# Sums of squares of the differential heads on column tiles, halvings spaced apart, and one head's norm factors taken later

## The chip, the core and the metric

The kernel runs on one core of a Trainium2 chip. The core has a matrix engine (TensorE, PE in the profile; PEld is its weight load), VectorE (DVE), ScalarE (ACT), GpSimd (POOL) and SyncE (SP), which here only starts DMA transfers. Each engine works through its own instructions in order, and engines wait for each other by semaphores. The metric is device time in microseconds (us) of one execution, as the median of several runs. The profile comes from one further execution.

## The reference

One decoder layer on 512 tokens of 1024 channels. The part that matters here is the differential attention: four heads, each with two softmax maps whose difference weights the values, followed by an RMS norm over the 128 value channels of that head.

```
p = softmax(scores)                               # (b, h, 2, q, s)
a = p[:, :, 0] - lam * p[:, :, 1]
out = einsum('bhqs,bshe->bqhe', a, v)             # 128 channels a head
out = rmsnorm(out, subln_g) * (1.0 - lam_init)
```

Beside it runs a modulation: `mod = silu(c) @ w_ada + b_ada` gives six rows of 1024 numbers (shift, scale, gate for each half of the layer). Before the attention there is a modulated norm and one input projection; a sliding-window attention, sigmoid gates, branch projections, an output projection, and a gated MLP with a short convolution complete the layer.

## The kernel before, in words

Matrix products of full precision are made of three products of halves of numbers (high x high, high x low, low x high; `mm3`, lines 130 to 132). Weights come in raw, ScalarE casts the high part and VectorE subtracts it for the low part (L126 and L127 in `split`).

The attention stages are written as a hand-set order on TensorE and POOL (a `manual_schedule` block); a scheduler orders DVE, ACT and SP by priorities and its own estimates of time. The clock of that written order is `fill(n)`: it emits n *ticks*, each three products of 512 columns for whatever projection is due (pq, pk and pw for queries, keys and values of later heads; pga and pgd for the gates; pA and pB for the branches). `after(n, fn)` has fn emitted n ticks later, `flush(kind)` emits what has been laid by under a name.

A differential head h goes through four query blocks n = 0 to 3. `diff_scores` makes the scores sd of one or two blocks on row tiles of 64 rows, `diff_softmax` the maps, `diff_transpose` turns them (td) and stores them as high and low parts (aTh, aTl). With all four turned, `diff_values` makes the head's output od, 128 channels by 512 tokens, channels on the partitions. ScalarE stores its squares (sq) and a scaled copy (of). The norm then has three steps, laid by for heads 0 to 2 and emitted during the next head:

- `stats` (list "sum", at n = 2): the sum of squares over the 128 channels for each token. Each of four blocks of 128x128 squares is loaded as weights and multiplied by one column of ones, so the sums (pss) come out with tokens on the partitions, one column a block. VectorE scales them by the softmax sum (dr) and makes a mean (ms); POOL raises it to the power -1/2 (L193).
- `end` (list "end", at n = 3): VectorE refines the root and makes the norm factors drs.
- `turn_norm` (list "norm", at n = 0 of the head after): four transposes (rb) spread the factors over the channels, VectorE multiplies, and a split stores the result outd.

For head 3 the same steps follow by counts of ticks (STAT_LAG, END_LAG, NORM_LAG). Head 2's factors are turned after the loop over blocks, between four ticks and od of head 3.

The modulation rows are computed beside this: `ada_rows` loads pieces of w_ada (ra) every eighth tick, and VectorE adds them up (arow), 128 partial sums of 1024 numbers for each of four rows. `ada_sum` then adds the partitions by halving: POOL starts seven DMA transfers that add the upper half of the partitions onto the lower (64, 32, ... 1), each after the one before has landed, and an eighth that writes the row to mod_rows in memory. They are emitted HALVE_LAG ticks apart. Rows 1 and 2 are read back into a tile m (L1079, on SP), which is turned on TensorE (pm) M2_LAG ticks after it was planned, and VectorE makes coefficients c of it. Behind the load of m on SP stand the last branch weights (wbd) and the output weights (wo), which VectorE multiplies by the first gate (L1135).

PSUM tiles named with `tbank` (tag t) share two buffers: pv, td, pss, rb and pm are all of this kind.

Of the kernel before, what the change touches and what calls it, by code (L numbers as in the profile page):

```python
# [8 lines left out]
F32 = mybir.dt.float32  # L9
# [5 lines left out]
P = 128  # L15
# [3 lines left out]
NT = S // P  # L19
# [9 lines left out]
ADA_AHEAD = 2  # L29
HP = 100000  # L30
ST = 6
HALVE_LAG = 6
ADA_EVERY = 8
ADA_EASY = 20

ROW_BEHIND = {0: -3, 4: -2}
ADA_START = 4
V_LAG = 13
M2_LAG = (48, 60)
STAT_LAG = 10  # L40
END_LAG = 3
NORM_LAG = 16
SWA_FILL = (2, 2, 5, 2, 2, 2, 2, 3)
DIFF_FILL = (3, 2, 4, 2)
# [14 lines left out]
def kernel(  # L59
# [22 lines left out]
    nc = tc.nc  # L82
# [3 lines left out]
    def pool(name, bufs=1, space=None, stack=ctx):  # L86
        kw = {} if space is None else {"space": space}
        return stack.enter_context(tc.tile_pool(name=name, bufs=bufs, reuse_waits="tile", **kw))
# [6 lines left out]
    def bank(tag, bufs, shape, name, dt=F32):  # L95
        return ps.tile(shape, dt, tag=tag, bufs=bufs, name=name)
# [4 lines left out]
    def sbank(name, shape=(P, S)):  # L101
        return bank("s", 3, list(shape), name)

    def tbank(name, shape=(P, S)):
        return bank("t", 2, list(shape), name)
# [28 lines left out]
    def mm3_rows(groups):  # L134
        for a, b, start, stop in ((0, 0, True, False), (0, 1, False, False), (1, 0, False, True)):
            for o, lhs, rhs in groups:
                nc.tensor.matmul(o, lhs[a], rhs[b], start=start, stop=stop)  # L137


    ones = cpool.tile([P, P], F32, name="ones")  # L140
    nc.gpsimd.memset(ones, 1.0)
    ident = cpool.tile([P, P], F32, name="ident")
# [347 lines left out]
    ap = pool("att", stack=at)  # L490
# [51 lines left out]
    def prefetch():  # L542
        while units and len(loaded) < 2:
            load, run = units.pop(0)
            loaded.append((load(), run))

    def fill(n):
        for _ in range(n):
            if not current:
                prefetch()  # L550
                if loaded and due[0]:
                    due[0] -= 1
                    wts, run = loaded.pop(0)
                    current.append(run(wts))
                    if tick[0]:
                        prefetch()
            if tick[0] == 7:
                prefetch()
            if current:
                try:  # L560
                    next(current[0])
                except StopIteration:
                    current.clear()
            for e in list(later):
                e[0] -= 1
                if e[0] <= 0:
                    later.remove(e)
                    e[1]()
            tick[0] += 1
            if tick[0] >= ADA_START and tick[0] % ADA_EVERY == 0:  # L570
                next(ada, None)

    beside = {"sum": [], "end": [], "norm": [], "turn": []}

    def after(n, fn):
        later.append([n, fn])

    def flush(*kinds):
        for kind in kinds:
            while beside[kind]:  # L580
                beside[kind].pop(0)()
# [148 lines left out]
    def diff_scores(*ss):  # L730
        ops = []
        for s in ss:
            h, n = divmod(s, NT)
            t = heads[h]
            w = (n + 1) * P
            if n == 0:
                firsts[h] = [sbank(f"sd{h}_{m}", (P, 2, 256)) for m in range(2)]
            sps = [
                firsts[h][m][:, n, :w] if n < 2 else (vbank if n + m == 4 else sbank)(f"sd{h}_{n}_{m}")[:, :w]
                for m in range(2)  # L740
            ]
            mm3_rows([
                (
                    sps[m],
                    [t[64 * m : 64 * m + 64, b, n * P : (n + 1) * P] for b in range(2)],
                    [t[64 * m : 64 * m + 64, 2 + b, :w] for b in range(2)],
                )
                for m in range(2)
            ])
            ops.append((s, sps, w))  # L750
        for s, sps, w in ops:
            h, n = divmod(s, NT)
            mx = ap.tile([P, 2], F32, tag="dmx", bufs=3, name=f"dmx{h}_{n}")
            pm = []
            for m in range(2):
                st = ap.tile([P, w], F32, tag="st", bufs=ST, name=f"sd{h}_{n}_{m}")
                with tc.high_priority(offset=HP):
                    maxima.append(nc.vector.tensor_tensor_reduce(
                        st, sps[m], ddf[:, 512 - w : 512], 1.0, -3e38, ALU.add, ALU.max, mx[:, m : m + 1]
                    ))  # L760
                pm.append(st)
            scored[s] = mx, pm
# [39 lines left out]
    def diff_values(h):  # L802
        t, (aTh, aTl) = heads[h], aTs[h]
        o = vbank(f"od{h}")
        for k in range(NT):
            q0 = k * P
            mm3(
                o[:, q0:], t[:, 4, k * P : (k + 1) * P], t[:, 5, k * P : (k + 1) * P],
                aTh[:, k * AW + q0 : k * AW + 512], aTl[:, k * AW + q0 : k * AW + 512],
                k == 0, k == NT - 1,  # L810
            )
        sq = ap.tile([P, S], F32, tag="tmp", bufs=2, name=f"sq{h}")
        of = ap.tile([P, S], F32, tag="of", bufs=2, name=f"of{h}")
        nc.scalar.activation(sq, o, AF.Square)
        nc.scalar.activation(of, o, AF.Copy, scale=sublnc)

        def stats():
            pss = tbank(f"pss{h}", (P, NT))
            for n in range(NT):
                nc.tensor.matmul(pss[:, n : n + 1], sq[:, n * P : (n + 1) * P], ones[:, 0:1], start=True, stop=True)  # L820
            rs, r0, r2 = (ap.tile([P, NT], F32, tag=t, bufs=2, name=f"{t}{h}") for t in ("drs", "dr0", "dr2"))
            nc.vector.reciprocal(r0, sums[h][:, 0])
            nc.vector.tensor_mul(r2, r0, r0)
            nc.vector.tensor_mul(r2, r2, pss)
            half = rstd_start(r2, NT, P, ap)

            def end():
                rstd_end(rs, *half, NT, ap)
                nc.vector.tensor_mul(rs, rs, r0)

            if h < 3:
                beside["end"].append(end)
            else:
                after(END_LAG, end)

            def turn_norm():
                rb = tbank(f"rb{h}")
                for n in range(NT):
                    nc.tensor.transpose(rb[:, n * P : (n + 1) * P], rs[:, n : n + 1].to_broadcast([P, P]), ident)
                with tc.high_priority(offset=HP):  # L840
                    nc.vector.tensor_mul(of, of, rb)
                split(outd[0][:, h], outd[1][:, h], of)

            if h < 3:
                beside["norm"].append(turn_norm)
            else:
                after(NORM_LAG, turn_norm)

        if h < 3:
            beside["sum"].append(stats)  # L850
        else:
            after(STAT_LAG, stats)


    mod_rows = tc.dram_tile([4, D], F32, name="mod_rows")
# [39 lines left out]
    def ada_sum(idx, whole):  # L895
        def step(n):
            if n:
                nc.gpsimd.dma_start(whole[0:n], whole[n : 2 * n], accum_op=ALU.add)  # L898
                after(HALVE_LAG, lambda: step(n // 2))
            else:  # L900
                nc.gpsimd.dma_start(mod_rows[idx : idx + 1], whole[0:1].rearrange("o a n -> o (a n)"))

        after(1, lambda: step(P // 2))
# [98 lines left out]
    for s in range(4 * DIFF_HEADS):  # L1002
        h, n = divmod(s, NT)
        if s in (4, 8):
            due[0] += 3
        elif s == 12:
            due[0] += 4
        ahead = s == 1
        fill(DIFF_FILL[1] - ahead)
        nxt = (s + 1, s + 2) if n % 2 and s < 15 else ()  # L1010
        if nxt:
            diff_scores(*nxt)
        if n == 3:
            with tc.issue_after(maxima[-1].ins):
                flush("end")
        if n == 1:
            diff_transpose(s)
        fill(DIFF_FILL[2] + ahead)
        if n == 2:
            flush("sum")  # L1020
        elif n == 0:
            flush("norm")
        if n != 1:
            diff_transpose(s)
        diff_softmax(*nxt)
        if n == 0 and h:
            diff_values(h - 1)
            fill(DIFF_FILL[3])
    due[0] += 2 * (KT - 4)
    fill(4)  # L1030
    flush("norm")
    diff_values(DIFF_HEADS - 1)
    while due[0] or current:
        fill(1)
    at.close()
# [52 lines left out]

    after(M2_LAG[0], load_m2)
    after(M2_LAG[1], turn_m2)  # L1090

# [270 lines left out]
    ssq, r2, xns = {}, {}, {}  # L1362
# [609 lines left out]
```

## Time and profile before

| what | us |
|---|---|
| median of the 3 runs shown (lowest, highest) | 690.01 (689.94, 692.77) |
| profiled execution, its own time | 691.2 |
| span of its instructions | 689.4 |
| TensorE busy | 677.5 (98%) |
| VectorE busy | 563.9 (82%) |
| ScalarE busy | 382.2 (55%) |
| GpSimd busy | 100.1 (15%) |

A row of the timeline has a start and a length in us from the span's start, the engine, the line of the source, the operation, what it writes and reads, its form, how many were merged into the row, and in brackets how long the engine was idle before it and what released it. Ends of products are modelled and overlap: a product with 512 columns is shown as 0.39 us long though the next one starts 0.23 us after it, so what a thing costs on TensorE is read from start to start. A window's row has the length, then busy time and instructions of PE, PEld, DVE, ACT and POOL, the TensorE clock granted, the share of the DMA engines, and GB/s.

The attention stages that the change touches lie between 110 and 235 us; from 235 to 308 us come gates and branches, then the output projection, and from 350 us the MLP.

### The profile page before, as it was taken

Reading aid. Unit: us, or ns where it says so; the run is one execution under the profiler, and the core shown is the slowest. Engines: PE = TensorE matmul, PEld = TensorE weight load, DVE = VectorE, ACT = ScalarE, POOL = GpSimd, SP = SyncE. Lnnn points to the kernel's source line nnn. Section 1 sums busy time; section 2 is a strip of 40 time slices with the busy share of each in tenths; the row PEclk is TensorE's granted clock in tenths of the full one; section 3 lists DMA queues with packets and bytes.
Section 4 is the critical chain, followed back from the end, with each engine's and each line's share of the span. In section 5 each row is a group of like instructions: output and inputs, shape, how many; then the busy total and the mean of one; then the engine's idle time right before and its main releaser. Section 6 shows DMA issues by size and latency. Waiting matters only on the chain.

```text
span 689.4 us, 11101 instructions
## 1 busy us (share of the span) xinstructions
PE 677.5 (98%) x4139; PEld 593.0 (86%) x4139; DVE 563.9 (82%) x1073; ACT 382.2 (55%) x678; POOL 100.1 (15%) x121
## 2 busy tenths in 40 slices
PE   8999999999989999999999999999999999999995
PEld 5887787888878888788899999999999999888885
DVE  5999775988775676793589988888888999979997
ACT  7676674546442323333377656655555666656665
POOL 3000000021012101111030011112110102440300
PEclk9999999999999999999999999999999999999998
DMA  9995412565455687569635788777979647995903
GB/s 306 351 295 180 131 61 76 166 167 157 139 145 160 215 256 201 170 175 327 216 67 119 181 209 191 170 168 216 208 212 220 155 161 182 196 205 144 168 1 122
DMA packets 116934, 123.89 MB, mean 180 GB/s; under 512 B 4983, under 2 KB 93848, under 8 KB 116880
## 3 DMA queue, kind: packets, MB, share of 16 engines
q1 hardware_dynamic: 97038, 95.11, 43.1%
q0 software_dynamic: 19648, 27.79, 23.8%
q8 instruction: 32, 0.52, 0.3%
q10 hardware_dynamic: 194, 0.28, 0.1%
q14 instruction: 22, 0.18, 0.1%
HBM read 118.97 MB, written 2.11 MB: 176 GB/s over the span
## 4 chain that ended last, share of the span: by engine, by line
PE 95%; DMA 2%; DVE 1%; ACT 0%; issue 0%; SPq 0%; POOL 0%; POOLq 0%; ACTq 0%
PE up L1300 32%; PE dc L1916 15%; PE a L393 5%; PE pgd L130 2%; PE pgd L131 2%; PE pgd L132 2%; PE oc L1356 2%; PE oc L1360 2%; PE oc L1357 2%; PE pga L130 2%; PE pga L132 2%; PE pga L131 2%; PE pq L130 1%; PE pw L130 1%; PE sd L137 1%; DMA adaw<-in_w_ada_dram 1%
## 5 line engine op out<-in xcount | busy, mean ns | idle before, releaser
L1300 PE MATMUL up<-t,m_whi 128*128 128x256 f32 x512 | 93.1, 283 | 0.0
L1300 PEld LDWEIGHTS up<-t,m_whi 128*128 128x128 f32 x512 | 79.9, 192 | 0.0
L1300 PE MATMUL up<-t,m_wlo 128*128 128x256 f32 x256 | 72.4, 283 | 0.0
L1300 PE MATMUL up<-bh,p_whi 128*128 128x256 f32 x232 | 65.7, 283 | 0.0
L1300 PE MATMUL up<-bl,p_whi 128*128 128x256 f32 x232 | 65.7, 283 | 0.0
L1300 PE MATMUL up<-bh,p_wlo 128*128 128x256 f32 x232 | 65.7, 283 | 0.0
L898 POOL DMA_DIRECT2D arow<-arow x28 | 22.6, 807 | 254.0 <-DVE sd L783 123.9
L1300 PEld LDWEIGHTS up<-t,m_wlo 128*128 128x128 f32 x256 | 49.2, 192 | 0.0
L1209 POOL DMA_DIRECT2D s<-in_w_up_dram x21 | 26.9, 1354 | 140.9 <-DMA s<-in_w_up_dram 58.9
L1300 PEld LDWEIGHTS up<-bh,p_whi 128*128 128x128 f32 x232 | 44.5, 192 | 0.0
L1300 PEld LDWEIGHTS up<-bl,p_whi 128*128 128x128 f32 x232 | 44.5, 192 | 0.0
L1300 PEld LDWEIGHTS up<-bh,p_wlo 128*128 128x128 f32 x232 | 44.5, 192 | 0.0
L890 DVE SCALAR_TENSOR_TENSOR arow<-ra,cs,arow 128x512 f32<-128x512 f32 x56 | 41.8, 748 | 0.4
L1237 ACT CAST m_whi<-s 128x1024 fp32r<-128x1024 f32 x31 | 32.5, 1049 | 11.1 <-DVE s L1231 6.3
L1241 DVE TENSOR_TENSOR m_wlo<-s,m_whi 128x1024 fp32r<-128x1024 f32 x31 | 37.8, 1219 | 0.0
L1300 PE MATMUL up<-t,p_whi 128*128 128x256 f32 x176 | 32.2, 283 | 0.0
L1300 PEld LDWEIGHTS up<-t,p_whi 128*128 128x128 f32 x176 | 27.5, 192 | 0.0
L1307 ACT ACTIVATE gT<-a,cv 128x512 f32<-128x512 f32 x22 | 17.7, 814 | 16.9 <-DVE a L1342 15.9
L1237 ACT CAST p_whi<-wa 128x1024 fp32r<-128x1024 f32 x18 | 18.8, 1043 | 12.5 <-PE up L1300 12.5
L193 POOL TENSOR_TENSOR r<-ms,mhalf 128x1 f32<-128x1 f32 (+1 forms) x16 | 13.1, 820 | 83.0 <-DVE ms L191 64.8
L1241 DVE TENSOR_TENSOR p_wlo<-wa,p_whi 128x1024 fp32r<-128x1024 f32 x18 | 22.0, 1223 | 3.8 <-ACT p_whi L1237 3.8
L1300 PE MATMUL up<-t,p_wlo 128*128 128x256 f32 x88 | 24.9, 283 | 0.0
(486 smaller groups left out, 2061.6 us busy)
## 6 DMA issues: line engine op xcount, KB each, us to landing
ra<-in_w_ada_dram SPq DMA_DIRECT2D x32, 512.0 KB, 4.3
wa<-in_w_up_dram SPq DMA_DIRECT2D x22, 512.0 KB, 4.6
s<-in_w_up_dram SPq DMA_DIRECT2D x21, 512.0 KB, 5.2
s<-in_w_up_dram POOLq DMA_DIRECT2D x21, 512.0 KB, 7.1
adaw<-in_w_ada_dram SPq DMA_DIRECT2D x12, 512.0 KB, 7.3
w<-in_w_in_dram SPq DMA_DIRECT2D x12, 512.0 KB, 4.9
a<-in_w_up_dram SPq DMA_DIRECT2D x11, 512.0 KB, 4.9
b<-in_w_down_dram SPq DMA_DIRECT2D x10, 512.0 KB, 4.9
```

The lines of the kernel that those rows point to most:

```text
L130: nc.tensor.matmul(o, lh, rh, start=start, stop=False)
L131: nc.tensor.matmul(o, lh, rl, start=False, stop=False)
L132: nc.tensor.matmul(o, ll, rh, start=False, stop=stop)
L393: nc.tensor.matmul(acc6[i], lhs[:, i * P : (i + 1) * P], rhs[k], start=k == 0 and p == 0, stop=last and p == 2)
L890: nc.vector.scalar_tensor_tensor(ac, r[:, a], cc, ac, ALU.mult, ALU.add)
L898: nc.gpsimd.dma_start(whole[0:n], whole[n : 2 * n], accum_op=ALU.add)
L1209: nc.gpsimd.dma_start(dst, upblock(*blk), accum_op=ALU.add)
L1237: nc.scalar.copy(W[J, name][0], R[J, SRC[name]])
L1241: nc.vector.tensor_sub(lo, R[J, SRC[name]], hi.bitcast(F32))
L1300: nc.tensor.matmul(o[u], w[:, k, cu], b[:, k], start=name in ("p1", "m5", "p2") and k == 0 and x == 0, stop=k == 3 and x == 2, skip_group_ ...
L1307: nc.scalar.activation(grow(j), av[J][:, u], AF.Identity, bias=cv[:, 66 + j : 67 + j], scale=cv[:, 44 + j : 45 + j])
L1916: nc.tensor.matmul(bank2[u][:, sl], a[:, q, cu], b[:, q, sl], start=first_mm and x == 0, stop=last_mm and x == 2, skip_group_check=name no ...
```

## The change

Sums of squares. `add_rows` is new: four products with a 128x32 block of ones as weights and 128 columns of squares, each on its own column tile of 32 columns (`tile_position`), so that token block g's sums stand on partitions 32g to 32g+31 of psr. ScalarE copies psr to ssrow; `stats` turns that tile once (pss) and reads columns 0, 32, 64 and 96. For heads 0 to 2 `add_rows` is emitted at n = 1 ahead of the scores, the turning where `stats` stood. For head 3 `add_rows` follows od by 7 ticks and the turning comes 3 ticks later, where one count of 10 stood before.

Third head's factors. `end` of head 2 is emitted after the loop and six ticks, then od of head 3, and `turn_norm` of head 2 eight ticks later.

Halvings. The first two gaps between the seven halvings grow from 6 ticks to 10 and 7. M2_LAG grows by 6.

```
-HALVE_LAG = 6
+HALVE_LAG = (10, 7, 6, 6, 6, 6, 6)
+LAST_NORM = 8
-M2_LAG = (48, 60)
-STAT_LAG = 10
+M2_LAG = (54, 66)
+STAT_LAG = 7
+TURN_LAG = 3
...
+        row = ap.tile([P, P], F32, tag="ssrow", name=f"ssrow{h}")
+        def add_rows():
+            pr = tbank(f"psr{h}", (P, P))
+            for g in range(4):
+                gs = slice(32 * g, 32 * g + 32)
+                nc.tensor.matmul(
+                    pr[gs], ones[:, gs], sq[:, g * P : (g + 1) * P], start=True, stop=True, tile_position=(0, 32 * g)
+                )
+            with tc.high_priority(offset=HP):
+                nc.scalar.copy(row, pr)
+            if h < 3:
+                beside["sum"].append(stats)
+            else:
+                after(TURN_LAG, stats)
...
-            pss = tbank(f"pss{h}", (P, NT))
-            for n in range(NT):
-                nc.tensor.matmul(pss[:, n : n + 1], sq[:, n * P : (n + 1) * P], ones[:, 0:1], start=True, stop=True)
+            pss = tbank(f"pss{h}", (P, P))
+            nc.tensor.transpose(pss, row, ident)
...
-            nc.vector.tensor_mul(r2, r2, pss)
+            with tc.high_priority(offset=HP):
+                nc.vector.tensor_mul(r2, r2, pss[:, 0:P:32])
...
-            beside["sum"].append(stats)
+            beside["row"].append(add_rows)
         else:
-            after(STAT_LAG, stats)
+            after(STAT_LAG, add_rows)
...
-                after(HALVE_LAG, lambda: step(n // 2))
+                after(HALVE_LAG[7 - n.bit_length()], lambda: step(n // 2))
...
+            if n == 1:
+                flush("row")
             diff_scores(*nxt)
-        if n == 3:
+        if n == 3 and nxt:
...
-    fill(4)
-    flush("norm")
+    fill(6)
+    flush("end")
     diff_values(DIFF_HEADS - 1)
+    after(LAST_NORM, lambda: flush("norm"))
```

Where this moves instructions. POOL, the powers (r) of the second, third and fourth head and the halvings (arow) of the second modulation row, before:

```order
L193 TENSOR_TENSOR r_2065<-ms,mhalf 128x4
L898 DMA arow_1680<-arow_1680 64x1024
L898 DMA arow_1680<-arow_1680 32x1024
L193 TENSOR_TENSOR r_2327<-ms,mhalf 128x4
L898 DMA arow_1680<-arow_1680 16x1024
L898 DMA arow_1680<-arow_1680 8x1024
L898 DMA arow_1680<-arow_1680 4x1024
L193 TENSOR_TENSOR r_2476<-ms,mhalf 128x4
```

and now:

```order
L195 TENSOR_TENSOR r_2072<-ms,mhalf 128x4
L919 DMA mod_rows<-arow_1051 16x1x64
L916 DMA arow_1680<-arow_1680 64x1024
L195 TENSOR_TENSOR r_2338<-ms,mhalf 128x4
L916 DMA arow_1680<-arow_1680 32x1024
L916 DMA arow_1680<-arow_1680 16x1024
L916 DMA arow_1680<-arow_1680 8x1024
L916 DMA arow_1680<-arow_1680 4x1024
L195 TENSOR_TENSOR r_2498<-ms,mhalf 128x4
```

The third head's power stands ahead of the halving of 32 partitions instead of behind it, and the second head's ahead of the write of the first row.

TensorE behind the last block of head 3, where head 2's factors were turned (rb) and od begins, before:

```order
L130 MATMUL pga_2375<-hThA,wga_h 128x512
L131 MATMUL pga_2375<-hTlA,wga_h 128x512
L132 MATMUL pga_2375<-hThA,wga_l 128x512
L839 MATMUL rb_2392<-ident,drs_2319 128x128 x4
L130 MATMUL od_2400<-aTh_2177,qkv_1879 128x512
```

and now the place where rb of head 2 stands, eight ticks behind od, one tick behind the sums of head 3:

```order
L825 MATMUL psr_2464<-sq_2423,ones 32x128 x4
L132 MATMUL pga_2460<-hThA,wga_h 128x512
L133 MATMUL pga_2460<-hTlA,wga_h 128x512
L134 MATMUL pga_2460<-hThA,wga_l 128x512
L857 MATMUL rb_2473<-ident,drs_2330 128x128 x4
```

Od follows gate products directly, and no four transposes of factors lie ahead of it.

VectorE near 284 us, where the coefficients c are made and the first output weights are multiplied by the gate, before:

```order
L1084 COPY c_2662<-pm_2961 128x40
L127 TENSOR_TENSOR mg1l<-tdall,mg1h 128x512
L1085 TENSOR_TENSOR c_2662<-c_2662 128x16
L890 SCALAR_TENSOR_TENSOR arow_2717<-ra_6_2907,cs,arow_2717 128x512
L1086 SCALAR_TENSOR_TENSOR c_2662<-c_2662 128x8
L1135 TENSOR_TENSOR wo_3147<-wo_3147,g1b 128x1024
```

and now:

```order
L1156 TENSOR_TENSOR wo_3163<-wo_3163,g1b 128x1024
L129 TENSOR_TENSOR mg1l<-tdall,mg1h 128x512
L908 SCALAR_TENSOR_TENSOR arow_2732<-ra_6_2922,cs,arow_2732 128x512
L1156 TENSOR_TENSOR wo_3170<-wo_3170,g1b 128x1024
L1105 COPY c_2678<-pm_2997 128x40
```

The first product with wo is ahead of what stood before it, and a second one is ahead of the copy of pm.

More of the change, by code (lines that the diff above doesn't have):

```diff
@@ L571, in fill @@
                 next(ada, None)
-    beside = {"sum": [], "end": [], "norm": [], "turn": []}
+    beside = {"row": [], "sum": [], "end": [], "norm": [], "turn": []}
     def after(n, fn):
```

## The prediction

> **What bounds the kernel now.** I read the page's busy shares and its chain first, then the waits of TensorE, then the stretch around the one long wait.
>
> ```profile
> PE 677.5 (98%) x4139; PEld 593.0 (86%) x4139; DVE 563.9 (82%) x1073; ACT 382.2 (55%) x678; POOL 100.1 (15%) x121
> PE 95%; DMA 2%; DVE 1%; ACT 0%; issue 0%; SPq 0%; POOL 0%; POOLq 0%; ACTq 0%
> ```
>
> TensorE is the bound: 95% of the chain is its own work. A change gains by less TensorE time or by closing one of its gaps. The longest gap in the view of waits is one that the change touches:
>
> ```profile
> PE rb L839 <- DVE drs L829: 1.9, 1, 1.9
> ```
>
> The timeline around it (start, length, engine, line, instruction), cut to the chain's rows:
>
> ```profile
> 196.04 0.88 POOL L898 DMA_DIRECT2D arow<-arow  x1 [20.01 <-DVE dr L822]
> 198.84 0.16 DVE L189 TENSOR_SCALAR ms<-dr 128x4 f32<-128x4 f32 x1
> 201.07 0.60 PE L797 MATMUL td<-ident,sd 128*128 128x128 f32 x4
> 203.08 0.78 POOL L898 DMA_DIRECT2D arow<-arow  x1 [6.16 <-DMA arow<-arow]
> 203.62 1.29 POOL L193 TENSOR_TENSOR r<-ms,mhalf 128x4 f32<-128x4 f32 x1
> 204.06 0.39 PE L132 MATMUL pga<-hThA,wga_l 128*128 128x512 f32 x1
> 205.43 0.68 DVE L499 TENSOR_TENSOR aTl<-td,aTh 128x512 fp32r<-128x512 f32 x1
> 206.32 0.71 PE L839 MATMUL rb<-ident,drs 128*128 128x128 f32 x4 [1.87 <-DVE drs L829]
> 207.26 0.63 PE L131 MATMUL od<-aTl,qkv 128*128 128x512 f32 x1
> 207.69 0.63 PE L132 MATMUL od<-aTh,qkv 128*128 128x512 f32 x1
> 210.21 0.44 PE L130 MATMUL pga<-hThA,wga_h 128*128 128x512 f32 x1
> ```
>
> The third head's mean square (ms) is ready at 199.0, but its power on POOL starts at 203.62: ahead of it in POOL's order stands the row's second halving (203.08), which waits 6.16 us for the first to land. So rb, and TensorE behind it, starts at 206.32. The product at 204.06 takes its place for 0.23 us (the spacing of its neighbours), so the gap is 206.32 - 204.29 = 2.03 us.
>
> It costs more than itself. Behind it the products od follow each other at 0.43 us (207.26 to 207.69). The head before reads:
>
> ```profile
> 182.82 0.60 PE L839 MATMUL rb<-ident,drs 128*128 128x128 f32 x4
> 183.60 0.39 PE L131 MATMUL od<-aTl,qkv 128*128 128x512 f32 x1
> 183.84 0.39 PE L132 MATMUL od<-aTh,qkv 128*128 128x512 f32 x1
> 185.23 0.45 PE L130 MATMUL pga<-hThB,wga_h 128*128 128x512 f32 x1
> ```
>
> There the spacing is 0.24, and from rb to the next gate product pass 2.41 us, against 3.89 behind the gap: 1.48 us more for the same work. The windows tell why (their last columns: granted clock, DMA share, GB/s):
>
> ```profile
> 198.00:204.20 6.20, 6.20 (x32) 5.00 (x31) 3.41 (x7) 2.97 (x4) 1.12 (x2) 1.00 0.96 277
> 206.30:210.10 3.80, 3.78 (x16) 3.51 (x16) 3.77 (x6) 0.62 (x1) 0.94 (x2) 0.56 0.41 67
> 210.10:214.00 3.90, 3.90 (x19) 3.27 (x19) 1.18 (x2) 1.99 (x4) 0.69 (x1) 0.99 1.00 281
> ```
>
> The granted clock is 1.00 before the gap, 0.56 for 3.8 us behind it, then 0.99.
>
> **The change, part by part.** *Halvings and the third head's norm.* POOL now has this power behind the issue of the first halving (196.04 plus 0.88) and ahead of the second. It can start with ms at 199.0, so the norm factors come some 4 us earlier, and rb asks for them eight ticks behind od, some 8 us later. The gap loses its cause: -2.03, and -1.48 of slow clock, together **-3.51 us**. The second halving waits for the first one's landing until 203.08 in any case, so the power (1.29) in front of it is free. The first two heads' powers now stand ahead of one halving and of the write of the first row, and hold these back by what they wait for ms. That row was done at 166.41 and the next halving started only at 196.04: slack of 29 us covers it.
>
> ```profile
> 166.41 0.53 POOL L901 DMA_DIRECT2D mod_rows<-arow  x1 [3.87 <-DMA arow<-arow]
> ```
>
> Late next is od, six ticks (18 products) behind td instead of four: 204.29 + 6 x 0.228 = 205.66. It needs aTl, made at 205.43 before because VectorE stood at the same power. With the power done at about 200.4, and three things of 0.6 to 1.2 us now ordered in front of aTl, that comes to about 204: cover of 1.5 us, nothing charged.
>
> *The squares.* Before, each head loads four blocks of squares as weights for one column each:
>
> ```profile
> 149.03 0.39 PE L132 MATMUL pw<-hThA,w_l 128*128 128x512 f32 x1
> 149.26 0.95 PE L820 MATMUL pss<-ones,sq 128*128 128x1 f32 x8
> 150.06 0.53 PE L797 MATMUL td<-ident,sd 128*128 128x128 f32 x3
> 150.35 0.48 PE L130 MATMUL pw<-hThA,w_h 128*128 128x512 f32 x1
> ```
>
> That holds TensorE for 150.06 - 149.26 = 0.80 us. Three transposes take 150.35 - 150.06 = 0.29, so the one that replaces it costs 0.10. New are four products on column tiles 32 wide: eight instructions of 128 columns, as each fp32 product shows as two. No row has four tiles; the nearest has two, 64 wide:
>
> ```profile
> 72.99 0.39 PE L132 MATMUL pw<-hThA,w_l 128*128 128x512 f32 x1
> 73.31 1.73 PE L675 MATMUL oa<-pT,va 128*64 128x256 f32 x16
> 74.97 0.50 PE L130 MATMUL pw<-hThA,w_h 128*128 128x512 f32 x1
> L675 PE MATMUL oa<-pT,va x64: 272/379/431, 73.3 to 109.8; 128*64 128x256 f32 x48, 128*64 128x128 f32 x16
> ```
>
> Sixteen instructions, twelve of 256 columns and four of 128, take 74.97 - 73.31 = 1.66 us: 0.463 ns a column with two tiles side by side. Ours have 1024 columns: 0.47 us in pairs, 0.24 if four run together, 0.95 if none do. The gap ahead of oa, 73.31 - 72.99 - 0.23 = 0.09, is taken as the price of a change of tiling. I take the pairs, the nearest row: 0.47 + 0.10 + 0.10 for the transpose = 0.67, a gain of 0.13 in each of three heads. The last head's squares stand amid gate products, with a change into and out of tiling: 0.77, the transpose with as much around it 0.2, against 0.80: +0.17. Sum -0.39 + 0.17 = **-0.2 us**. Ends: with four together 0.23 a head better, -1.1; with none 0.48 worse, +1.7.
>
> [...]
>
> *The rest.* ScalarE copies four more tiles of 128x128; it is 55% busy and the sums are asked for two to four ticks later: nothing charged. If a copy is late, the transpose is. The tile of sums takes a further PSUM buffer of the pair that the transposes use; td then waits for one use further back, which was drained already.
>
> The matrix m is loaded in the same place of SP's queue, and turned six ticks (4.2 us) later, which covers a TensorE that runs 3.7 us ahead of a load that stays. But VectorE's order there changes, and this is where a gain can be lost:
>
> ```profile
> SPq L1079 <- DMA mod_rows<-arow: 8.7, 1, 8.7
> 247.59 0.86 POOL L898 DMA_DIRECT2D arow<-arow  x1 [19.16 <-DVE arow L890]
> 281.34 0.33 SPq L1079 DMA_DIRECT2D m<-mod_rows  x1
> 283.02 0.24 PE L1083 MATMUL pm<-ident,m 40*128 40x40 f32 x1
> 284.02 0.20 DVE L1084 COPY c<-pm 128x40 f32<-128x40 f32 x1
> 285.49 0.16 DVE L1086 SCALAR_TENSOR_TENSOR c<-c 128x8 f32<-128x8 f32 x1
> 286.58 1.22 DVE L1135 TENSOR_TENSOR wo<-wo,g1b 128x1024 f32<-128x1024 f32 x1 [0.94 <-DMA wo<-in_w_out_dram]
> 298.80 1.23 DVE L127 TENSOR_TENSOR wbd<-wbd,wbd 128x1024 fp32r<-128x1024 f32 x1
> 302.63 0.39 PE L130 MATMUL pB<-outdA,wbd 128*128 128x512 f32 x1
> ```
>
> SP stands 8.7 us for the third row's sums before it loads m, and the output weights wo are queued behind. VectorE's first product with wo waits for that load (0.94). It now comes before the work of 284.02 to 285.65, so 1.63 us more lie behind the load. The low part of wbd ends at 300.03 and is wanted at 302.63 + 2 x 0.23 = 303.09: slack 3.06, now 1.43. If the load moves ahead with TensorE, that holds. The row's halvings began at 247.59 on VectorE's release, and its work there follows TensorE, so I take it to move and charge nothing.
>
> Sum: -3.51 - 0.2 = **-3.7 us**. The profiled execution took 691.2 for a span of 689.4, so the sum says 687.5 there; the median of the runs shown, 690.01, is 1.2 lower, and gives **686.3 us**.
>
> **The rivals.**
>
> *Tiles one after another* (+1.7 instead of -0.2): 690.0 - 3.5 + 1.7 = 688.2. Were their loads exposed too, at the 0.80 / 8 = 0.10 of a load and its column in the squares' row, 3.2 more: 691.4, the far end. For it speaks that no row shows four tiles, against it that two ran together.
>
> *Only the gap comes back.* If the slow 3.8 us belonged to something other than the gap, or came in another place, 2.03 + 0.2 return: 687.8. The windows, 1.00 then 0.56 right behind the gap, speak against it. [...]
>
> *VectorE late at wbd* (the other side). If the load of wo stays at its time while TensorE comes 3.7 earlier, the low part is late by 3.7 - 1.43 = 2.3 us. A gap of 2.03 cost 1.48 of clock, so 3.8 go: 690.1, all given back. It decides from there: each us that the third row lands later than now makes the kernel slower by one, and with 3.5 it is 693.6. The 8.7 us that SP waits show how much hangs on that row.
>
> *The gap moves to od.* If aTl is still late by 2 us, gap and clock stay: 689.8. Against it, cover of 1.5 us.
>
> **How the numbers follow.** My forecast, 685.3 to 687.0 with the four-tile bounds, has 0.62; serial tiles 0.13; only the gap 0.05; od late 0.06; VectorE late 0.14, half of it at or below 690 and half above. A measurement of this kernel tells 0.5%, 3.45 us, from no change. Below 686.56 lies most of the forecast, 0.55; above 693.46 about half of the last rival's upper half and what I don't see, 0.07; between them 0.38. The likeliest time is 686.3; the range goes from 685.0 (four tiles together, 685.4, and a little) to 689.8, which leaves out the late VectorE's upper part.
>
> **What would show it.** Right: no wait of rb on drs; a granted clock near 1.00 from 204 to 212 with od spaced 0.23; POOL's third power of this stage starting at about 199; the sums and their transpose at 0.6 to 0.8 us a head. Wrong: psr of 0.95 or more; a new wait of PE on td, od or wbd; a window of clock near 0.56 anywhere between 200 and 310; VectorE idle for a load of wo by more than 2 us.

## The result and the profile after

The changed kernel took 686.97 us (median of 7 runs, 686.19 to 687.82) beside 689.94 us of the kernel before: a ratio of 0.9947, with a 95% interval of 0.9933 to 0.9962. A later comparison of the same two kernels gave 686.07 beside 689.59 and 0.9946 (0.9931 to 0.9961). The forecast was 686.3 us, 0.7 below what was measured. Of the three terms behind it, though, two were far off, in opposite directions. That is what the rest is about.

The page after, its busy times and its chain, and from the view of waits the one row of TensorE that had no match before:

```profile
PE 674.5 (98%) x4143; PEld 588.8 (86%) x4143; DVE 564.1 (82%) x1073; ACT 381.2 (56%) x682; POOL 100.1 (15%) x121
PE 92%; DMA 4%; DVE 2%; issue 1%; ACT 1%; SPq 0%; POOLq 0%; ACTq 0%; DVEq 0%
PE oc L1377 <- DVE tdall L1087: 0.3, 1, 0.3
```

TensorE is 3.0 us less busy (677.5 before, which holds a stretch of slow clock; 676.0 to 676.9 in three later profiles of before) and still the bound. The wait of rb on drs, 1.9 us before, is gone. A short one at the output projection (oc) is new.

The timeline after, first the squares of the first head, then the place of the former wait:

```profile
140.97 0.43 PE L825 MATMUL psr<-sq,ones 128*32 128x128 f32 x8
141.33 1.49 PE L139 MATMUL sd<-qkv 64*128 64x384 f32 x12
...
149.86 0.27 PE L837 MATMUL pss<-ident,ssrow 128*128 128x128 f32 x1
149.96 0.49 PE L799 MATMUL td<-ident,sd 128*128 128x128 f32 x3
150.21 0.48 PE L132 MATMUL pw<-hThA,w_h 128*128 128x512 f32 x1
...
195.27 0.83 POOL L916 DMA_DIRECT2D arow<-arow  x1 [18.32 <-DVE dls L783]
198.63 1.03 POOL L195 TENSOR_TENSOR r<-ms,mhalf 128x4 f32<-128x4 f32 x1 [2.53 <-DVE ms L191]
200.74 0.82 POOL L916 DMA_DIRECT2D arow<-arow  x1 [1.08 <-DMA arow<-arow]
204.45 0.39 PE L134 MATMUL pga<-hThA,wga_l 128*128 128x512 f32 x1
204.68 0.39 PE L132 MATMUL od<-aTh,qkv 128*128 128x512 f32 x1
```

The third head's power runs on POOL at 198.63, five microseconds earlier than before (203.62) and between the two halvings. Od follows the gate products at the usual 0.23 us. Four products of sums take 141.33 - 140.97 = 0.36 us, their transpose 0.10.

The windows after (length; busy time of PE, PEld, DVE, ACT, POOL; granted clock, DMA share, GB/s) show full clock on both sides of that place, where the profile before had 0.56 behind it:

```profile
198.00:204.20 6.20, 6.20 (x30) 5.08 (x29) 4.94 (x13) 2.55 (x4) 1.86 (x2) 1.00 1.01 276
206.30:210.10 3.80, 3.80 (x20) 3.21 (x20) 1.24 (x3) 2.71 (x4) 0.81 (x1) 1.00 0.89 263
```

Executions differ in their first 100 us by some tenths (in one case by 3.8 us), so spans alone compare badly. I cut each profile at three starts: the first product sd of the differential heads, the first product pB behind the attention, and TensorE's last product. For the changed kernel these are

```profile
110.26 0.95 PE L139 MATMUL sd<-qkv 64*128 64x128 f32 x12
247.71 0.39 PE L132 MATMUL pB<-outdA,wbd 128*128 128x512 f32 x1
677.72 0.28 PE L1937 MATMUL dc<-p4wh,p4a 128*128 128x256 f32 x1
```

or 137.45 us from sd to pB and 430.01 from pB to the end. The same differences for every kernel (the experiments are below):

| profiled execution | sd to pB | pB to the end | TensorE's clock behind rb |
|---|---|---|---|
| before, the profile of the prediction | 142.51 | 429.45 | half for 3.4 us |
| before, again / third / fourth | 140.79 / 140.56 / 140.74 | 429.43 / 429.54 / 429.43 | full |
| after / after again | 137.45 / 137.45 | 430.01 / 429.39 | full |
| order alone | 138.92 | 429.57 | full |
| squares alone | 139.14 | 429.86 | full |
| seven fillers | 139.61 | 429.83 | full |
| one filler | 144.72 | 429.72 | half for 3.4 us |
| one column tile | 141.56 | 429.36 | full |
| two column tiles | 138.79 | 429.36 | full |
| wo behind arow, twice | 137.45 / 137.44 | 429.38 / 429.40 | full |

Against the mean of the three ordinary executions of before (140.70), the change saves 3.25 us between sd and pB. Behind pB the first profile after loses 0.5 us against before (429.47), the second nothing. The 0.3 to 0.4 us that squares alone and the two fill kernels stand longer there is a wait of 0.3 us at the turning of the modulation rows (pm), which each of their three profiles has and no other.

### The profile page after: what moved, and what is told of

It is laid out like the page before. It is cut to its first block, busy times and chain, and to the rows that moved or that the text cites. A ratio compares the mean times of both kernels' runs of the same rounds, so it can differ in the third digit from the quotient of the medians.

```text
span 685.2 us, 11115 instructions
## 1 busy us (share of the span) xinstructions
PE 674.5 (98%) x4143; PEld 588.8 (86%) x4143; DVE 564.1 (82%) x1073; ACT 381.2 (56%) x682; POOL 100.1 (15%) x121
## 4 chain that ended last, share of the span: by engine, by line
PE 92%; DMA 4%; DVE 2%; issue 1%; ACT 1%; SPq 0%; POOLq 0%; ACTq 0%; DVEq 0%
PE up L1321 32%; PE dc L1937 15%; PE a L395 5%; DMA wo<-in_w_out_dram 3%; PE pga L132 2%; PE pga L134 2%; PE pga L133 2%; PE oc L1377 2%; PE oc L1378 2%; PE oc L1381 2%; PE sd L139 1%; PE pgd L133 1%; PE pgd L134 1%; PE pgd L132 1%; PE pq L132 1%; PE pw L132 1%
## 5 line engine op out<-in xcount | busy, mean ns | idle before, releaser
L780 ACT ACTIVATE sd<-sd,dmx 128x128 f32<-128x128 f32 (+3 forms) x32 | 17.7, 556 | 17.3 <-DVE dmx L770 17.3
```

The source lines that it names most:

```text
L780: exp = nc.scalar.activation(pm[m], pm[m], AF.Exp, bias=mx[:, m : m + 1], scale=slope, accum_out=ls)
```

## The experiments

Each run stands with its edit, against the kernel before unless it says otherwise.

### The order alone

```
-HALVE_LAG = 6
+HALVE_LAG = (10, 7, 6, 6, 6, 6, 6)
+LAST_NORM = 8
...
-M2_LAG = (48, 60)
+M2_LAG = (54, 66)
...
-                after(HALVE_LAG, lambda: step(n // 2))
+                after(HALVE_LAG[7 - n.bit_length()], lambda: step(n // 2))
...
-        if n == 3:
+        if n == 3 and nxt:
...
-    fill(4)
-    flush("norm")
+    fill(6)
+    flush("end")
     diff_values(DIFF_HEADS - 1)
+    after(LAST_NORM, lambda: flush("norm"))
```

> The order part alone: halvings' lags 10, 7, 6, 6, 6, 6, 6, the third head's norm factors behind six fillers, the M2 turn six ticks later; the squares stay the 16 one-column products of before. Theory (gap account): the 2.03 us wait at rb and the 1.48 us of half clock behind it go, no wait comes at rb or od, the granted clock is 1.00 from 200 to 214 us; VectorE's instructions around the first products wo by g1b stand in the same order as in the changed kernel, so about 0.4 us of wait comes back at the output projection (oc): -3.5 + 0.4 = about -3.1 us, 686.9 us beside 690.0. Rival 'the squares carry the gain': -1.5 us or less. Rival 'clock drop has nothing to do with the gap': -2.0 us, with half clock still there for about 3.4 us.

Measured: 687.63 us beside 689.69, ratio 0.9970 (0.9959 to 0.9981); -2.06 us by the medians, where the gap account expected -3.1. No wait at rb or od; from sd to pB 140.70 - 138.92 = 1.78 us less, which is a wait and no half clock. The wait at oc that I expected from VectorE's order did not come.

### The squares alone

```
-STAT_LAG = 10
+STAT_LAG = 7
...
+TURN_LAG = 3
...
+            pr = tbank(f"psr{h}", (P, P))
+            for g in range(4):
+                gs = slice(32 * g, 32 * g + 32)
...
+            nc.tensor.transpose(pss, row, ident)
...
```

> The squares part alone: sums by four products on column tiles into psr and one transpose into pss, with the lags that the changed kernel gives them; halvings, third head's norm factors and M2 turn as before, so the wait at rb stays. Theory A (what ends the wait moves with TensorE): the four heads save 0.3 to 0.4 us each, 1.2 to 1.5 us in sum, and the wait stays 2.0 us: -1.2 us, 688.8. Theory B (the end of the wait is fixed by the halving's transfer and does not move): the 0.8 to 1.0 us saved ahead of rb only make the wait longer (2.8 to 3.0 us), and what is left is the last head's 0.2 to 0.4 us: -0.3 us, 689.7. Rival 'column tiles run one after another': +0.1 to +0.3 us a head, slower by 0.5 to 1 us.

Measured: 688.20 us beside 689.69, ratio 0.9974 (0.9963 to 0.9984): -1.5 us, and 1.56 less from sd to pB. That is theory A, and a little more. The timeline of this kernel at rb:

```profile
201.57 0.78 POOL L915 DMA_DIRECT2D arow<-arow  x1 [5.61 <-DMA arow<-arow]
202.11 1.30 POOL L194 TENSOR_TENSOR r<-ms,mhalf 128x4 f32<-128x4 f32 x1
202.91 0.39 PE L133 MATMUL pga<-hThA,wga_l 128*128 128x512 f32 x1
204.81 0.62 PE L856 MATMUL rb<-ident,drs 128*128 128x128 f32 x4 [1.52 <-DVE drs L846]
205.19 0.48 PE L131 MATMUL od<-aTh,qkv 128*128 128x512 f32 x1
205.51 0.40 PE L132 MATMUL od<-aTl,qkv 128*128 128x512 f32 x1
205.74 0.40 PE L133 MATMUL od<-aTh,qkv 128*128 128x512 f32 x1
```

TensorE still waits, 204.81 - 203.14 = 1.67 us, for the same power behind the same halving; the end of the wait moved ahead with TensorE. But od follows at 0.23 us: a wait, and no half clock behind it. This row made me doubt the 1.48 us of clock in the forecast.

The two parts add up: 1.78 + 1.56 = 3.34, beside 3.25 for both.

### Seven fillers

```
-    fill(4)
+    fill(7)
     flush("norm")
```

> The kernel before with one number changed: seven fillers in place of four ahead of the third head's norm factors, so nine more products of 0.23 us (2.1 us) stand on TensorE ahead of rb and cover the wait; the halvings, squares, M2 turn and the order of VectorE's work near 284 us are as before. Gap account: the wait at rb goes to 0 to 0.1 us and the half clock behind it with it: -3.5 us, 686.5 us, with no new wait at the output projection. Rival (the clock drop follows from something else than the wait): -2.0 us, 688.0, half clock still there. Rival (od, the next wait, takes the place): -2 to -1 us.

Measured: 688.51 us beside 689.69, ratio 0.9987 (0.9978 to 0.9996): -1.2 us, less than the gap account and its first rival expected. It lies within the -2 to -1 of the last rival, but od does not wait. The wait at rb is gone, and so is any half clock. A new wait opens on TensorE further on. The value products of head 3 now come in a closer place, and a gate product has to wait:

```profile
211.98 0.39 PE L132 MATMUL pA<-outah,wba_l 128*128 128x512 f32 x1
212.77 0.50 PE L130 MATMUL pga<-hThA,wga_h 128*128 128x512 f32 x1 [0.40 <-ACT ta L911]
```

The gate product starts 0.79 us behind its neighbour instead of 0.23, since ScalarE makes squares and copy of od (1.06 us by their starts) ahead of ta. That takes 0.56 of the 1.77 back. Covering a wait with work from behind it is worth the wait less what that work is missed for.

### The kernel before, three times more

No edit.

> The kernel before, profiled once more. The runs of the parts do not add up as the prediction had them: the order alone gave -2.06 us, the squares alone -1.5 us, seven fillers -1.2 us by their medians, and in the profile with the squares alone TensorE waits 1.5 us at rb without a half clock behind it. Theory 'the half clock comes in few executions': the wait at rb is 1.9 us again and the mean clock behind it is 1.00, the products of od follow each other at 0.23 us, and the time is 689.0 to 690.0 us. Rival 'the half clock belongs to every execution of the kernel before': 0.50 for about 3.4 us behind rb, mean clock 0.994, as in the first profile.

> The kernel before, profiled a third time, for how often the half clock follows the wait of 1.9 to 2.0 us at rb: of three waits so far (2.03, 1.87 and 1.67 us from the end of the product ahead to rb) only the longest had it, and one of 4.0 us had it too. Theory 'a threshold near 1.9 to 2.0 us': half clock if the wait is 2.0 or more, none if it is below 1.9. Rival 'where the wait falls against a window that runs on its own decides': either outcome at any of these lengths.

> The kernel before, profiled a fourth time, with the same two theories as the run beside it: a wait of 2.0 us or more with half clock and one below 1.9 without would speak for the threshold; a wait of below 1.9 with half clock, or one of 2.0 or more without, for the window that runs on its own.

Measured: 689.11, 689.59 and 689.47 us. The waits at rb, from the end of the product ahead (its start plus 0.23), were 1.87, 1.64 and 1.81 us. None had a half clock behind it. That fits the threshold, since none of them reached 1.9, and it does not contradict the rival; one more step on this follows with the next run. The windows behind rb, of the second and the fourth profile:

```profile
206.30:210.10 3.80, 3.80 (x23) 3.36 (x22) 3.78 (x7) 1.35 (x3) 1.09 (x2) 1.00 0.49 111
```

```profile
206.30:210.10 3.80, 3.80 (x23) 3.41 (x23) 3.77 (x6) 1.00 (x2) 1.05 (x2) 1.00 0.41 74
```

So the profile from which I predicted was the unusual one. It took 691.2 us; less the 1.48 of slow clock that is 689.7, and the median of the 35 runs of before in the two longest comparisons is 689.64. In those 35 the mean clock was 0.994 once (691.46 us) and 0.996 to 0.998 otherwise, while 3.41 us at half clock lower the mean by 3.41 x 0.5 / 689 = 0.0025. A few of the 0.996 may hide such a stretch; most runs had none.

### One filler

```
-    fill(4)
+    fill(1)
     flush("norm")
```

> The kernel before with one filler in place of four ahead of the third head's norm factors: nine products of 0.23 us fewer ahead of rb, so that the wait there is 2.0 + 2.1 = 4.1 us, if its end does not move. Theory 'a long enough wait brings the half clock, one of 2 us seldom': half clock for about 3.4 us behind rb, then in every execution; the nine products are done later at full speed, so the time is 689.7 + 2.1 + 1.5 = 693.3 us. Rival 'the half clock does not follow from the wait': clock 1.00 and 691.8 us.

Measured: 693.57 us, and the half clock is there. The windows of the wait, of the first 0.6 us behind it, and of what follows:

```profile
203.00:206.10 3.10, 0.00 (x0) 0.02 (x1) 1.29 (x6) 0.14 (x1) 1.71 (x2) 1.00 0.84 199
206.10:206.70 0.60, 0.59 (x5) 0.60 (x6) 0.60 (x2) 0.00 (x0) 0.01 (x1) 1.00 0.00 0
206.80:210.10 3.30, 3.30 (x13) 3.09 (x12) 3.28 (x5) 0.67 (x2) 0.94 (x2) 0.50 0.49 92
210.20:214.00 3.80, 3.80 (x18) 3.09 (x18) 0.95 (x2) 1.03 (x2) 0.47 (x1) 1.00 0.81 233
```

The wait was 4.00 us (the product ahead started at 201.88, rb at 206.11). In the first profile of before, cut in the same way, TensorE starts at 206.32 and reads

```profile
206.30:206.70 0.40, 0.38 (x4) 0.40 (x5) 0.40 (x1) 0.00 (x0) 0.00 (x0) 1.00 0.00 0
206.74:210.14 3.40, 3.40 (x14) 3.11 (x13) 3.37 (x6) 0.62 (x1) 0.98 (x2) 0.50 0.47 81
```

In both the clock stays full for the first 0.4 to 0.7 us of work, is exactly 0.50 for 3.4 us, and full again. So the half clock goes with the wait in both, and the rival that it is a thing of its own would need chance twice. It rests on one execution with each of these two waits.

What decides at 1.6 to 2.0 us (waits of 1.64, 1.67, 1.81 and 1.87 had no half clock, one of 2.03 had it) can be read in part from the times at which the granted clock changes, found with narrow windows. In the profile of before it falls at 206.73, in that of one filler at 206.77, and in one of wo held back, further down, at 12.09. The last fall, behind TensorE's last product, comes at 684.60, 688.05 and 684.52. The two falls of an execution thus lie 477.87, 481.28 and 672.43 us apart. In before the half clock lasts 3.41 us (206.73 to 210.14), and 140, 141 and 197 steps of 3.4133 us give the three distances; the step is my estimate from these times. Behind rb the half clock did not begin when work resumed but 0.41 us later in before (206.73 - 206.32) and 0.66 in one filler (206.77 - 206.11), in both a whole number of these steps ahead of the last fall. Points laid back at that step from an execution's last fall make a grid. The stretches between two points that held the wait, in the profiles of before, before again (its grid laid back from the last fall at 684.76) and one filler:

```profile
203.32:206.73 3.41, 1.54 (x10) 1.01 (x9) 1.71 (x6) 0.00 (x0) 1.59 (x2) 1.00 0.68 158
203.48:206.89 3.41, 1.70 (x10) 1.22 (x9) 2.38 (x7) 0.00 (x0) 1.27 (x2) 1.00 0.57 118
203.36:206.77 3.41, 0.66 (x5) 0.68 (x6) 1.96 (x7) 0.00 (x0) 1.42 (x3) 1.00 0.67 154
```

TensorE is busy for 1.54 and 0.66 us where the clock fell, for 1.70 where it did not. The waits of 2.03 and 1.87 us each lie wholly inside one stretch, and only the longer had half clock behind it; that of 1.81 in the fourth profile, which had none, is cut in two by a point at 205.32 (its grid laid back in the same way). Between the first two the length differs; whether the place of a wait counts too is not shown. Nor is a sharp limit: busy times are modelled, and the fall at 12.09 followed a stretch with 1.77 us busy, more than the 1.70 with no fall behind it.

### One column tile, two column tiles

Against the changed kernel: the four products all on column tile 0 (32 columns wide, four stretches of PSUM, four transposes of 32 rows), or on two tiles of 64 columns (two transposes).

```
-                gs = slice(32 * g, 32 * g + 32)
+                gs = slice(g * P, g * P + P)
...
-                    pr[gs], ones[:, gs], sq[:, g * P : (g + 1) * P], start=True, stop=True, tile_position=(0, 32 * g)
+                    pr[0:32, gs], ones[:, 0:32], sq[:, gs], start=True, stop=True, tile_position=(0, 0)
...
```

```
-                gs = slice(32 * g, 32 * g + 32)
+                gs = slice(64 * (g % 2), 64 * (g % 2) + 64)
...
-                    pr[gs], ones[:, gs], sq[:, g * P : (g + 1) * P], start=True, stop=True, tile_position=(0, 32 * g)
+                    pr[gs, g // 2 * P : (g // 2 + 1) * P], ones[:, gs], sq[:, g * P : (g + 1) * P],
+                    start=True, stop=True, tile_position=(0, 64 * (g % 2)),
...
```

> The changed kernel with the four products of a head's squares all on one column tile of 32 (the same 32 rows of the sum, four stretches of PSUM), so that they can't run side by side; then four transposes of 32 rows in place of one of 128. Prices from psr to the next instruction on TensorE: four tiles at once took 0.36 us. Theory 'the four tiles run at once': one tile takes four times as long for the part that streams, 0.9 to 1.0 us a head, +0.5 to +0.7 us a head with the transposes, +2 us in all: 689 us. Rival 'the tiles bring nothing, the short weight load does': 0.36 to 0.45 us again, and no more than +0.3 us in all.

> The changed kernel with the four products on two column tiles of 64 columns (two products behind each other on each), and two transposes of 128 rows. Theory 'tiles run at once as many as there are': about 0.47 to 0.55 us from psr to the next instruction, between the 0.36 of four tiles and the 0.9 to 1.0 of one; with the second transpose +0.2 us a head, +0.8 us in all: 687.8 us. Rival 'only pairs run at once, so four tiles are no better than two': 0.36 us again.

Measured: 690.15 us with one tile, 687.43 with two, one execution each. The sums of the first head, with one tile:

```profile
140.67 1.06 PE L825 MATMUL psr<-sq,ones 128*32 128x128 f32 x8
141.66 1.49 PE L139 MATMUL sd<-qkv 64*128 64x384 f32 x12
L825 PEld LDWEIGHTS psr<-sq,ones x32: 106/110/110, 140.7 to 214.9; 128*32 128x32 f32 x32
```

and with two:

```profile
140.72 0.66 PE L825 MATMUL psr<-sq,ones 128*64 128x128 f32 x8
141.31 1.49 PE L139 MATMUL sd<-qkv 64*128 64x384 f32 x12
L825 PEld LDWEIGHTS psr<-sq,ones x32: 132/137/137, 140.7 to 212.5; 128*64 128x64 f32 x32
```

From psr to sd the eight instructions take 0.99 us on one tile, 0.59 on two and 0.36 on four. The first theory fits nearly: two tiles take 0.59 / 0.99 = 0.60 and four 0.36 / 0.99 = 0.36 of one tile's time, where running wholly side by side would give 0.50 and 0.25. On one tile an instruction costs 0.99 / 8 = 0.124 us, a little more than its weight load of 0.110: the eight loads alone fill 0.88 of the 0.99, so even there the products run beside loads. On four tiles eight loads of 0.106 to 0.110, in sum at least 0.85, and eight products pass in 0.36, so there the loads of different tiles run beside each other as well. From sd to pB two tiles cost 1.34 us more than four and stand where the old squares stood (138.79 beside 138.92). One tile costs 4.1 more, twice the 2 us expected: of about 1.0 in each head 0.63 is in the sums, and 0.39 in the four transposes of 32 rows and the changes around them.

### wo behind arow

Against the changed kernel: VectorE's products of wo by the gate are held behind the last sum of arow.

```
...
+                        summed[:] = [nc.vector.scalar_tensor_tensor(ac, r[:, a], cc, ac, ALU.mult, ALU.add)]
...
-        nc.vector.tensor_mul(r, r, gate)
+        with tc.issue_after(summed[-1].ins):
+            nc.vector.tensor_mul(r, r, gate)
```

The profile after had shown where the time behind pB went:

```profile
282.15 1.22 DVE L1156 TENSOR_TENSOR wo<-wo,g1b 128x1024 f32<-128x1024 f32 x1 [2.83 <-DMA wo<-in_w_out_dram]
...
302.21 1.23 DVE L1156 TENSOR_TENSOR wo<-wo,g1b 128x1024 f32<-128x1024 f32 x1 [0.85 <-DMA wo<-in_w_out_dram]
...
307.19 0.68 DVE L1087 SCALAR_TENSOR_TENSOR tdall<-tdall,pB 128x512 f32<-128x512 f32 x1
307.92 0.50 PE L1377 MATMUL oc<-wo_h,mg0h 128*128 128x512 f32 x1 [0.26 <-DVE tdall L1087]
```

VectorE waits for landings of wo, its last sum with pB ends at 307.87, and the product oc that takes over pB's PSUM starts at 307.92, 0.4 us late.

> The changed kernel with one thing added: VectorE's products of wo by the gate g1b are held behind the last arow sum, so that no landing of wo stands ahead of the arow sums that free the buffers of the next loads. Theory (the wait of 0.42 us in the output projection at 307.9 us, on VectorE's sum of tdall, comes from VectorE waiting 2.8 us for the first wo at 279.3 us, which delays the fourth load of wo from about 281 to 286.9 us): the fourth load is issued 4 to 6 us earlier, the wait at oc goes, 0.4 to 0.7 us faster than the changed kernel: 686.3 us, ratio to the kernel before 0.994. Rival (the loads of wo are limited by the transfers themselves): the wait stays, same as the changed kernel, 687.0. Rival (something else is pushed out, such as the halving of arow): a wait near 298 us at wbd or for c, 687.5.

> The changed kernel once more, beside the same kernel with VectorE's products of wo held behind the arow sums (next run), on one chip. About 0.995 of the kernel before, with the wait at oc of 0.3 us and the eight loads of wo issued over about 20 us.

> The changed kernel with VectorE's products of wo by the gate held behind the last arow sum, beside the changed kernel on one chip. By the profiles, from the first product pB to TensorE's last product 429.38 us against 430.01: theory 0.6 us faster than the changed kernel in this call, by the medians. Rival (the difference of the medians, 686.97 against 686.11, was that of the chips): the same within 0.2 us.

Measured: first 686.11 us beside 689.69, ratio 0.9948 (0.9936 to 0.9960); then, on one chip, 686.34 us beside 686.07 for the changed kernel, with ratios to before of 0.9955 (0.9940 to 0.9970) and 0.9946 (0.9931 to 0.9961). The first run has the time that the theory gave, but beside the changed kernel on one chip nothing is left of the gain (0.27 us the other way), so the rival is right about the time. The wait of 0.3 us at oc that I expected again in the changed kernel did not come either. The mechanism itself is there. The row of sums in the two kernels, the changed one again and then the one with wo held back:

```profile
305.59 0.68 DVE L1087 SCALAR_TENSOR_TENSOR tdall<-tdall,pB 128x512 f32<-128x512 f32 x1
307.32 0.39 PE L1377 MATMUL oc<-wo_h,mg0h 128*128 128x512 f32 x1
```

```profile
303.46 0.68 DVE L1087 SCALAR_TENSOR_TENSOR tdall<-tdall,pB 128x512 f32<-128x512 f32 x1
307.54 0.39 PE L1378 MATMUL oc<-wo_h,mg0h 128*128 128x512 f32 x1
```

The sum ends 307.32 - 306.27 = 1.05 us ahead of its use in the one, and 307.54 - 304.14 = 3.4 us in the other; in the first profile after it was too late. SP's eight loads of wo spread over 20.1 and 19.8 us in the changed kernel, 17.6 and 18.1 with wo held back. The second profile after has about 1 us of cover there; in the first, where VectorE's last wait for wo is 0.85 us and not 0.21, it is used up. How often that happens isn't settled; the medians show it seldom.

## Why the prediction was right, and where not

**The wait at rb.** Right in cause and nearly in size. The power behind the second halving was what held rb; put ahead of it, it started at 198.63 (forecast: about 199), and the wait went, with none at od. It was sized at 2.03 us from the one profile. Three more have 1.64 to 1.87, and the order alone gave 1.78 between sd and pB.

**"and -1.48 of slow clock".** This step failed. The 1.48 us was real in the profiled execution, and the one filler has 3.4 us of half clock behind a wait too (4.00 us). But I took it off the median, which did not contain it: the three other profiles of before have full clock behind rb. The warning stood in the prediction's own sum: the profiled execution was 1.2 us above the median, and this stretch explains that. The rival "only the gap comes back" had the right price for most runs, though for another cause, and I gave it 0.05.

**"I take the pairs, the nearest row".** The term of the sum that was mis-sized. Four tiles run together: 0.36 us where I took 0.47 + 0.10 = 0.57. Each of three heads gained 0.41 us where I had 0.13: td of head 3's last block starts 201.07 - 109.99 = 91.08 us behind the first sd before (the same 91.08 in all four profiles) and 200.11 - 110.26 = 89.85 after, 1.23 for three. The first sd before and that td after:

```profile
109.99 0.95 PE L137 MATMUL sd<-qkv 64*128 64x128 f32 x12
200.11 0.60 PE L799 MATMUL td<-ident,sd 128*128 128x128 f32 x4
```

The last head gained 0.24 where I had a loss of 0.17. In all 1.47 us (138.92 - 137.45) instead of 0.2, beyond the end of 1.1 that I gave for four tiles together. The price of 0.24 for four, plus the 0.10 that I allowed for a change of tiling, would have come within 0.02 of the measured 0.36; the two-tile kernel's 0.59 is as near to the pairs' 0.57. The scaling was right, and the choice of row wrong. The first head checks it by rows: from pss to the next projection product passed 150.35 - 149.26 = 1.09 us before and 150.21 - 149.86 = 0.35 now, and 0.36 for the sums makes a gain of 0.38. In the last head the sums cost 0.45 us with the change of tiling ahead of them (from 211.13 + 0.23 to 211.81) and the transpose 0.11, where I had 0.77 and 0.2; the change behind them was in the old squares' surroundings already. My 0.77 also held 0.10 too much: 0.47 and two changes of 0.10 make 0.67.

**VectorE near 284 us, nothing charged.** Right in the median, and right that the load of m moves ahead with TensorE (277.20 against 281.34). The cover that I named did shrink, and by more than I had: the low part of wbd ends at 297.89 and is wanted at 298.25, 0.36 us later (0.7 in the second profile after), where it had 3.06 and I expected 1.43.

```profile
296.67 1.22 DVE L129 TENSOR_TENSOR wbd<-wbd,wbd 128x1024 fp32r<-128x1024 f32 x1
298.25 0.39 PE L134 MATMUL pB<-outdA,wbd 128*128 128x512 f32 x1
```

That just held. The wait came at another cover, which I had not named: that of the PSUM that oc takes over from pB. It was 3.7 us before (VectorE's sum ended at 309.11; oc started at 308.23, and asks for that PSUM 4.57 us later, as it does undisturbed in the second profile after: 307.32 - 302.75) and about 1 or none after. My sign for it, VectorE idle for a load of wo by more than 2 us, did show (2.83).

**The sum.** Forecast 3.51 + 0.2 = 3.7. The profiles give 1.78 + 1.47 = 3.25 between sd and pB, and 0 to 0.5 back behind it; the medians give 2.97 and 3.52. The total was right because 1.48 too much for the clock, with 0.25 too much for the wait, and 1.27 too little for the squares nearly cancel. That is luck. The range's lower end and the 0.55 for a time below 686.56 rested on that as well, and the measured 686.97 lies above it.

## What to carry to other kernels

If the profiled execution is longer than the median, look in it for what the median lacks, and take a gain off the median only after that is out; here three of four profiles of the same kernel would have told. Column tiles ran side by side here, four of 32 columns in 0.36 us where one took 0.99, although all used the same rows, so sums over partitions with a narrow result are worth trying on four. A wait that is covered by moved work, or a load that is consumed earlier in the queue, was paid for here in cover elsewhere (0.56 of 1.77 us with seven fillers): list the next user of each buffer (here ta on ScalarE, and the PSUM of pB) before counting the whole of it, and measure how much of each cover is left: here 0.36 us at wbd.

## What the runs showed that I had not expected

The wait of 2.03 us was followed by 3.4 us of half clock that began only 0.4 us after work had resumed, 140 steps of 3.41 us ahead of the execution's last fall of the clock, and nearly equal waits (1.87, 1.81) by none. The first 20 us had a half clock once: in one profiled execution of the kernel with wo held back, TensorE waited 2.5 us for VectorE's xn, in two parts of 0.88 and 1.61 (not at all in the other profile of that kernel), then had the clock at 0.52 and 0.62 from 12 to 16 us. Its first sd started at 113.63 instead of about 110; of that the half clock can hold 1.7 at most. That execution took 689.76 us where the seven others took 685.84 to 687.93:

```profile
12.00:14.00 2.00, 2.00 (x11) 2.00 (x11) 1.72 (x7) 1.97 (x3) 0.46 (x1) 0.52 1.09 364
14.00:16.00 2.00, 2.00 (x14) 2.00 (x13) 0.73 (x3) 0.93 (x2) 0.00 (x0) 0.62 1.14 343
```

Apart from such stretches the time from sd to pB repeats to 0.01 us (137.44 to 137.45 in four executions of two kernels with the same order on TensorE), which made differences of tenths readable that the medians could not resolve.
